# Norms by blocks of two and four tiles, squares of the residual added up by TensorE, S5 tables without zero blocks

## The chip, the cores and the metric

The kernel runs on one core of one Trainium2 chip. The metric is the time of one execution in microseconds (us) on the device. The kernel is written in Bass with the Tile framework, whose scheduler gives every engine its list of instructions from the program's order and from priorities.

## The reference

The program is one inference step of a decoder of two layers, on a prompt of 512 tokens and on 8 sequences of 4 new tokens that share the weights; the width D is 1024. Each layer is:

```
h = rms_norm(x, g_mix_pre)
p = h @ w_in                      # split into four head groups
m = concat(rwkv7(p1), s5(p2), gated_delta(p3), sliding_window_attention(p4))
x = x + rms_norm(m @ w_out, g_mix_post)
h = rms_norm(x, g_mlp_pre)
x = x + rms_norm(square(relu(h @ w_up)) @ w_down, g_mlp_post)

def rms_norm(x, g):
    return x * lax.rsqrt(jnp.mean(x * x, axis=-1, keepdims=True) + 1e-6) * g
```

The S5 group is a complex diagonal state space model: 16 groups of 16 channels, 64 states each, with input and output matrices B and C for each group. The outputs are the two results and all states of the four mixers.

## The kernel before

**Halves.** The 544 columns (tokens) are worked off in two halves: half 0 has 256 columns of the prompt, half 1 the other 256 and the 32 columns of the samples, 288. A vector x is kept transposed, as 8 tiles of 128 rows (features) by n columns; a norm's sum over features is therefore a sum over tiles on one engine, and then over partitions by a product with `mean`, a column of 1/D that is broadcast to 128x128.

**Dense products.** `dense` goes over units of 128 output rows. A unit's weights come in two half-units [128, 4, 128] (`load_part`, issued by SP, line 1658, five buffers `wraw`). ScalarE rounds each to `whi`, VectorE subtracts to get `wlo` (three buffers each), the input is split likewise (`h[0]`, `h[1]`), and three products (hi*hi, hi*lo, lo*hi) over eight tiles make 24 matmuls a unit. All matmuls have the one line 219 (`mm`). The other helpers are `tt` (two tensors, line 235), `stt` (tensor, scalar, tensor, line 244), `act` (line 227) and `acopy` (line 231, copies and casts on ScalarE).

**Norms.** `square_sum` squares one tile on ScalarE and has GpSimd add it to `sums`; `rms` multiplies by `mean` and takes the root on ScalarE (Ln, then Exp). `prenorm` makes h for the next dense product: for each of 8 tiles one `stt` (x times weight times root), one cast, one subtraction. `residual` does for each tile one `stt` (output times weight times root), one `tt` (add the old x, which comes by DMA from DRAM, one tile at a time into the class `xk`), and `square_sum` of the new x; in the last layer it takes whole buffers. Its temporaries and the squares share the class `d1`, two buffers.

**S5.** `s5_tables` makes for each layer the tables kin, m1 and m2 and stores them in DRAM; `s5_main`, once for each half and layer, loads them (`halves`, `table`, line 1439, classes r4 and r2, five buffers each) and forms products of 128x128 blocks with the inputs U and the states H. Two groups of 64 rows share a block, and the blocks off the diagonal hold zeros. A float32 matmul shows as two instructions of TensorE.

**Order.** `body` writes out the order: project and mixers of a half, `out_proj`, `mlp`. A residual is put into `pending` (`later`) and popped inside the next dense product, ahead of its second and third unit, with the priority 'norm'; `flush` pops at once. Thus mix (0,0) is the residual after the output projection of layer 0, half 0, and mlp (0,1) that after the MLP of layer 0, half 1. There are eight: mix and mlp for two layers and two halves; mlp (1,0) and (1,1) are final and write the result.

**Buffers.** `CLS` gives each class its bytes per partition and its buffers: h9, f9 and acc are whole inputs of 8 tiles, two buffers each; xs has one. h9 holds the inputs of projections and of the MLP, f9 the MLP's inner activations or the input of the next layer's projection.

Of the kernel before, what the change touches and what calls it, by code (L numbers as in the profile page):

```python
# [9 lines left out]
F32 = mybir.dt.float32  # L10
# [9 lines left out]
HA = 288  # L20
# [4 lines left out]
NORM_EPS, RW_LN_EPS = 1e-6, 64e-5  # L25

# [112 lines left out]
class K:  # L139
# [21 lines left out]
    CLS = {"c0": (640, 7), "c1": (1152, 4), "e1": (1280, 2), "d1": (1152, 2), "xk": (1152, 3), "sums": (1152, 3),  # L161
# [1094 lines left out]
    def s5_tables(self, l):  # L1256
# [51 lines left out]
        misc = self.w([128, 2, 512], "r4")  # L1308
        bx, cx = (self.view(misc[:, j], [128, 2, 8, 2, 16]) for j in range(2))
# [14 lines left out]
        for out, pq, a, b, c, d in ((kx, rv, bb[:, 0], bb[:, 1], bb[:, 1], bb[:, 0]),  # L1324
                                    (m1, pw[:, :, 1:5], bc[:, 1, 0], bc[:, 1, 1], nbc[:, 1], nbc[:, 0])):
            for x, (u, v) in enumerate(((a, b), (c, d))):
                for y, w in enumerate((u, v)):
                    self.tt(tmp[:, y], over(w), pq[:, y].rearrange("q j a -> q a j").unsqueeze(2).to_broadcast([128, 8, 16, 4]), eng=e)
                for g2 in range(2):
                    rs = slice(64 * g2, 64 * g2 + 64)  # L1330
                    self.tt(out[x][rs, :, g2], tmp[rs, 0], tmp[rs, 1], ALU.add if x else ALU.subtract, eng=e)
        for g2 in range(2):
            rs = slice(64 * g2, 64 * g2 + 64)
            for x in range(2):
                nc.gpsimd.tensor_copy(bx[rs, x, :, g2], bb[rs, x])
            nc.gpsimd.tensor_copy(cx[rs, 0, :, g2], bc[rs, 1, 0])
            nc.gpsimd.tensor_copy(cx[rs, 1, :, g2], nbc[rs, 1])
        tab = [self.t([128, n], f"s5{nm}{l}", pool="dram", bufs=1) for nm, n in (("kin", 2048), ("m1", 2048), ("m2", 1024))]
        for x in range(2):
            self.nc.sync.dma_start(out=tab[1][:, x * 1024:x * 1024 + 1024], in_=m1[x].rearrange("p a b c d -> p (a b c d)"))  # L1340

        gps = []
        for q in range(2):
            gp = self.ps([128, 4, 2, 4, 16])
            for e in range(4):
                w = 4 * q + e
                for x in range(2):
                    lt = bx[:, x, w].rearrange("p a c -> p (a c)")
                    self.mm(gp[:32, e, :, 0], lt, cx[:, x, w], x == 0, False)
                    self.mm(gp[:32, e, :, 1:4], lt, m1[x][:, w, :, :, 0:3].rearrange("p g h j -> p g j h"), False, x == 1)  # L1350
            gps.append(gp)
        ga = self.w([32, 8, 2, 4, 16], "s0")
        for q in range(2):
# [680 lines left out]
```

## Time and profile before

| | |
|---|---|
| median of 3 runs | 1672.88 us (1667.75 to 1679.4) |
| profiled execution | 1675.07 us, span 1673.3 us, mean granted clock of TensorE 0.966 |
| TensorE | 1576.6 us busy, 94% of the span |
| VectorE | 1245.0 us, 74% |
| ScalarE | 952.2 us, 57% |
| GpSimd | 373.9 us, 22% |
| read from and written to HBM | 243.20 MB, 31.21 MB |

PE is TensorE's matmul part, PEld its weight load, DVE VectorE, ACT ScalarE, POOL GpSimd, SP the engine that issues most DMAs. A busy time is the union of an engine's instructions; the mean of one instruction overlaps its neighbours on TensorE, so there the busy time divided by the count, or the distance of two starts, is what one costs.

### The profile page before, as it was taken

Reading aid. Unit: us, or ns where it says so; the run is one execution under the profiler, and the core shown is the slowest. Engines: PE = TensorE matmul, PEld = TensorE weight load, DVE = VectorE, ACT = ScalarE, POOL = GpSimd, SP = SyncE. Lnnn points to the kernel's source line nnn. Section 1 sums busy time; section 2 is a strip of 40 time slices with the busy share of each in tenths; the row PEclk is TensorE's granted clock in tenths of the full one; section 3 lists DMA queues with packets and bytes.
Section 4 is the critical chain, followed back from the end, with each engine's and each line's share of the span. In section 5 each row is a group of like instructions: output and inputs, shape, how many; then the busy total and the mean of one; then the engine's idle time right before and its main releaser. Section 6 shows DMA issues by size and latency. Waiting matters only on the chain. (4 is left out here: it accounts for less than half of the span.)

```text
span 1673.3 us, 38301 instructions
## 1 busy us (share of the span) xinstructions
PE 1576.6 (94%) x14098; PEld 1472.2 (88%) x14098; DVE 1245.0 (74%) x3067; ACT 952.2 (57%) x2096; POOL 373.9 (22%) x689
## 2 busy tenths in 40 slices
PE   6988998789999999989999998999999999899996
PEld 6877987679898999879989998989899899899996
DVE  7888675876696868898576667989778865966665
ACT  5676556744346467765453556886444456655543
POOL 6561142200122614530001004530002101400002
PEclk9998998879999999999999999999999899999998
DMA  6634453343467557736346455535544765555452
GB/s 219 221 120 118 140 165 123 108 119 117 135 189 252 179 170 231 234 105 167 106 152 196 165 179 191 172 126 144 145 140 146 234 209 187 194 189 166 160 169 98
DMA packets 210184, 275.21 MB, mean 164 GB/s; under 512 B 78266, under 2 KB 101116, under 8 KB 209580
## 3 DMA queue, kind: packets, MB, share of 16 engines
q1 hardware_dynamic: 208076, 266.59, 50.8%
q0 software_dynamic: 1920, 6.17, 1.0%
q8 instruction: 110, 1.80, 0.4%
q14 instruction: 78, 0.64, 0.1%
HBM read 243.20 MB, written 31.21 MB: 164 GB/s over the span
## 5 line engine op out<-in xcount | busy, mean ns | idle before, releaser
L231 ACT CAST whi<-wraw 128x512 fp32r<-128x512 f32 x752 | 463.5, 619 | 439.3 <-PE ps L219 268.4
L235 DVE TENSOR_TENSOR wlo<-wraw,whi 128x512 fp32r<-128x512 f32 x752 | 545.7, 730 | 198.5 <-ACT whi L231 171.3
L219 PE MATMUL ps<-h,whi 128*128 128x288 f32 (+1 forms) x3264 | 518.6, 299 | 20.1 <-ACT h L231 17.8
L219 PEld LDWEIGHTS ps<-h,whi 128*128 128x128 f32 x3264 | 455.4, 194 | 35.2 <-ACT h L231 22.1
L219 PE MATMUL ps<-f,whi 128*128 128x288 f32 (+1 forms) x2752 | 425.6, 294 | 9.6 <-ACT whi L231 4.7
L219 PEld LDWEIGHTS ps<-f,whi 128*128 128x128 f32 x2752 | 374.4, 190 | 22.4 <-ACT whi L231 6.8
L219 PE MATMUL ps<-h,wlo 128*128 128x288 f32 (+1 forms) x1632 | 291.0, 298 | 7.4 <-DVE wlo L235 6.8
L219 PEld LDWEIGHTS ps<-h,wlo 128*128 128x128 f32 x1632 | 238.7, 193 | 16.1 <-DVE wlo L235 11.2
L219 PE MATMUL ps<-f,wlo 128*128 128x288 f32 (+1 forms) x1376 | 238.7, 293 | 3.3 <-DVE wlo L235 3.1
L235 POOL TENSOR_TENSOR sums<-sums,d 128x288 f32<-128x288 f32 (+1 forms) x105 | 101.8, 970 | 548.9 <-ACT d L227 541.0
L219 PEld LDWEIGHTS ps<-f,wlo 128*128 128x128 f32 x1376 | 197.4, 190 | 8.5 <-DVE wlo L235 4.6
L219 PE MATMUL ps<-r,r 128*128 128x72 f32 (+7 forms) x800 | 90.0, 281 | 4.5 <-DVE r L235 2.6
L219 PEld LDWEIGHTS ps<-r,r 128*128 128x128 f32 (+4 forms) x800 | 72.3, 175 | 11.0 <-DVE r L235 3.3
L235 DVE TENSOR_TENSOR acc<-acc,ps 128x256 f32<-128x256 f32 (+1 forms) x96 | 41.7, 434 | 49.5 <-PE ps L219 49.1
L231 ACT CAST f<-d 128x256 fp32r<-128x256 f32 (+1 forms) x136 | 56.6, 416 | 29.1 <-DVE d L235 28.5
L227 ACT ACTIVATE d<-acc 128x288 f32<-128x288 f32 (+1 forms) x109 | 46.2, 431 | 34.5 <-DVE acc L235 20.9
L235 DVE TENSOR_TENSOR f<-d,f 128x256 fp32r<-128x256 f32 (+1 forms) x136 | 59.1, 436 | 6.8 <-ACT f L231 6.7
L235 DVE TENSOR_TENSOR d<-d 128x288 f32<-128x288 f32 (+1 forms) x128 | 58.1, 454 | 0.7 <-ACT d L227 0.7
L227 ACT ACT_TABLE_LOAD x43 | 55.2, 1283 | 0.8
L227 ACT ACTIVATE d<-ps 128x288 f32<-128x288 f32 (+1 forms) x128 | 50.4, 394 | 8.8 <-PE ps L219 8.0
L244 DVE SCALAR_TENSOR_TENSOR d<-acc,pf,sums 128x256 f32<-128x256 f32 (+1 forms) x80 | 39.7, 507 | 6.2 <-ACT sums L227 4.9
L231 ACT COPY r<-ps 64x128 f32<-64x128 f32 (+2 forms) x60 | 22.7, 383 | 27.3 <-PE ps L624 11.4
(381 smaller groups left out, 1861.9 us busy)
## 6 DMA issues: line engine op xcount, KB each, us to landing
wraw<-in_w_up SPq DMA_DIRECT2D x256, 256.0 KB, 2.8
wraw<-in_w_down SPq DMA_DIRECT2D x256, 256.0 KB, 2.9
wraw<-in_w_in SPq DMA_DIRECT2D x176, 256.0 KB, 3.0
wraw<-in_w_out SPq DMA_DIRECT2D x64, 256.0 KB, 2.9
r<-s5m SPq DMA_DIRECT2D x12, 512.0 KB, 5.2
t<-diag SPq DMA_DIRECT2D x32, 128.0 KB, 3.2
r<-s5kin SPq DMA_DIRECT2D x8, 512.0 KB, 5.2
x<-acc SPq DMA_DIRECT2D x3, 1152.0 KB, 5.5
```

What stands on the lines that cost most here:

```text
L219: return self.nc.tensor.matmul(out=out, lhsT=lhsT, rhs=rhs, start=start, stop=stop)
L227: return self.nc.scalar.activation(out=out, in_=in_, func=func, scale=scale, bias=bias, **kw)
L231: return self.nc.scalar.copy(out, in_)
L235: return (eng or self.nc.vector).tensor_tensor(out=out, in0=a, in1=b, op=op)
L244: return self.nc.vector.scalar_tensor_tensor(out=out, in0=a, scalar=s, in1=b, op0=op0, op1=op1)
```

## The change

Five things change. (1) `prenorm` multiplies blocks of two tiles by the root on VectorE; ScalarE then applies the weight while it rounds, and VectorE's `stt` gives the low part. (2) `residual` works on blocks of four tiles (two where it is final), takes x in two DMAs of four tiles into a larger class, and the weights g_mix_post and g_mlp_post are applied before it, by ScalarE, in `out_proj.out` and in `mlp.down`. (3) For five of the six residuals that are not final, ScalarE squares blocks of four tiles and eight products with `mean` add them up, and no GpSimd add is left there. In all other sums the add of the last tile goes to VectorE. (4) S5's tables have no zero blocks any more, and their products are made in two 64x64 quadrants. (5) The table building works on the smaller tables.

```diff
@@ CLS
-"xk": (1152, 3)
+"d2": (2304, 2)
@@ s5_tables
-        kx, m1 = ([self.w([128, 8, 2, 16, 4], "r4") for _ in range(2)] for _ in range(2))
-        for tl in (*kx, *m1, bx, cx):
-            nc.gpsimd.memset(tl, 0.0)
+        kx, m1 = (self.w([128, 2, 8, 16, 4], "r4") for _ in range(2))
+        nc.gpsimd.memset(bx, 0.0)
...
-                for g2 in range(2):
-                    rs = slice(64 * g2, 64 * g2 + 64)
-                    self.tt(out[x][rs, :, g2], tmp[rs, 0], tmp[rs, 1], ALU.add if x else ALU.subtract, eng=e)
+                self.tt(out[:, x], tmp[:, 0], tmp[:, 1], ALU.add if x else ALU.subtract, eng=e)
...
-                    self.mm(gp[:32, e, :, 0], lt, cx[:, x, w], x == 0, False)
-                    self.mm(gp[:32, e, :, 1:4], lt, m1[x][:, w, :, :, 0:3].rearrange("p g h j -> p g j h"), False, x == 1)
+                self.mm(gp[:32, w, 0], lt, (bc[:, 1, 0] if not x else nbc[:, 1])[:, w], x == 0, False)
+                self.mm(gp[:32, w, 1:4], lt, m1[:, x, w, :, 0:3].rearrange("p h j -> p j h"), False, x == 1)
...
-                for e in range(4):
-                    self.tr(tp[:, e], kx[x][:, 4 * q + e].rearrange("p a b c -> p (a b c)"))
-                self.acopy(kin[:, 4 * q:4 * q + 4], tp)
-            self.nc.sync.dma_start(out=tab[0][:, x * 1024:x * 1024 + 1024], in_=kin.rearrange("p a c -> p (a c)"))
+            for q in range(4):
+                self.tr(tp[:, q], kx[:, x, 2 * q:2 * q + 2].rearrange("p a b c -> p (a b c)"))
+            kin = self.w([128, 4, 128], "r2")
+            self.acopy(kin, tp)
+            for e in range(2):
+                for g2 in range(2):
+                    self.nc.sync.dma_start(out=kt[64 * g2:64 * g2 + 64, x, :, e], in_=kin[64 * e:64 * e + 64, :, 64 * g2:64 * g2 + 64])
...
@@ s5_main
-        kin = halves(tkin)
+        kin = table(self.w([128, 2, 8, 64], "r4"), tkin)
-                    self.mm(p[:, e], kin[g0 // 4][:, x, e], U[:, g0 + e])
+                    for rs in GROUPS:
+                        self.mm(p[rs, e], kin[rs, x, g0 + e], U[rs, g0 + e])
-        m1, m2 = halves(tm1), table(self.w([128, 8, 128], "r4"), tm2)
+        m1, m2 = table(self.w([128, 2, 8, 64], "r4"), tm1), table(self.w([128, 8, 64], "r2"), tm2)
-                self.mm(yp[:, e], m2[:, w], U[:, w], True, False)
+                for rs in GROUPS:
+                    self.mm(yp[rs, e], m2[rs, w], U[rs, w], True, False)
                 for x in range(2):
-                    self.mm(yp[:, e], m1[g0 // 4][:, x, e], H[x][:, w], False, x == 1)
+                    for rs in GROUPS:
+                        self.mm(yp[rs, e], m1[rs, x, w], H[x][rs, w], False, x == 1)
@@ square_sum
-        self.tt(sums, sums, sq, ALU.add, eng=self.nc.gpsimd)
+        self.tt(sums, sums, sq, ALU.add, eng=self.nc.gpsimd if m < 7 else None)
@@ prenorm
-        for k in range(8):
-            t = self.row(half, "c1" if half and self.last_layer else "d1")
-            self.stt(t, x[:, k], self.p(g)[:, k:k + 1], rs)
-            self.parts(h[0][:, k], h[1][:, k], t)
+        for q in range(0, 8, 2):
+            u = self.w([128, 2, HA], "r2" if half and self.last_layer else "d2")[:, :, :n]
+            self.tt(u, x[:, q:q + 2], rs.unsqueeze(1).to_broadcast([128, 2, n]))
+            for k in (q, q + 1):
+                gk = self.p(g)[:, k:k + 1]
+                self.act(h[0][:, k], u[:, k - q], AF.Copy, scale=gk)
+                self.stt(h[1][:, k], u[:, k - q], gk, h[0][:, k].bitcast(F32), ALU.mult, ALU.subtract)
@@ residual
+    def fetch(self, half, cls):
+        if cls == "r4":
+            xt = [self.w([128, 4, HALVES[half][1]], "r4") for _ in range(2)]
+        else:
+            t = self.big(half, cls)
+            xt = [t[:, 0:4], t[:, 4:8]]
+        for q in range(2):
+            self.nc.sync.dma_start(out=xt[q], in_=self.x[half][:, 4 * q:4 * q + 4])
+        return xt
...
-            t = self.row(half, "c1" if whole else "d1")
-            self.stt(t, src[:, k], self.p(g)[:, k:k + 1], rs)
-            self.tt(src[:, k], t, xk, ALU.add, eng=self.nc.gpsimd if final and k % 2 else None)
-            if not final:
-                self.square_sum(new, k, src[:, k])
+        step = 2 if final else 4
+        for q in range(0, 8, step):
+            a, xq = src[:, q:q + step], xt[q // 4][:, q % 4:q % 4 + step]
+            self.tt(a, a, rs.unsqueeze(1).to_broadcast([128, step, n]))
+            self.tt(a, a, xq, ALU.add, eng=self.nc.gpsimd if final and q == 2 else None)
+            if final:
+                self.nc.sync.dma_start(out=self.o["yT"][:, q:q + step, c0:c0 + n], in_=a)
+            elif wide:
+                self.act(xq, a, AF.Square)
+                mp = self.ps([128, n], "mn") if mp is None else mp
+                for k in range(4):
+                    m = self.mm(mp, self.mean.to_broadcast([128, 128]), xq[:, k], q + k == 0, q + k == 7)
             else:
+                for k in range(4):
+                    self.square_sum(new, q + k, a[:, k])
...
-        return new
+        return self.rsqrt(new, mp, m) if wide else self.rms(new)
@@ out_proj.out
-            self.acopy(o[:, m], ps)
-            self.square_sum(sums, m, o[:, m])
+            self.square_sum(sums, m, ps)
+            self.act(o[:, m], ps, AF.Copy, scale=self.p("g_mix_post")[:, m:m + 1])
@@ out_proj
+        cls = {(0, 0): "f9", (0, 1): "h9", (1, 0): "r4", (1, 1): "xs"}[l, half]
+        self.later(lambda: x.update(rs=self.residual(half, o, sums, cls, wide=(l, half) != (0, 1))))
@@ mlp.down, after the last sum of squares
+                self.act(acc[:, m], acc[:, m], AF.Copy, scale=self.p("g_mlp_post")[:, m:m + 1])
@@ mlp
+        self.later(lambda: r.update(s=self.residual(half, acc, sums, ("xs" if half else "r4") if final else "f9", final)))
```

## Rows read from the trace of the kernel before

**Rows 1.** The page, part 1: engine, busy us, share of the span, instructions.

```profile
PE 1576.6 (94%) x14098; PEld 1472.2 (88%) x14098; DVE 1245.0 (74%) x3067; ACT 952.2 (57%) x2096; POOL 373.9 (22%) x689
```

**Rows 2.** Waits of PE: what for, us in total, times, longest.

```profile
PE ps L219 <- ACT h L231: 17.8, 10, 3.6
...
PE ps L219 <- POOL sums L235: 7.9, 3, 4.4
...
PE ps L219 <- DMA r<-s5m: 1.2, 1, 1.2
```

**Rows 3.** Windows: length, busy us of PE, PEld, DVE, ACT, POOL; clock, DMA, GB/s.

```profile
340.00:360.00 20.00, 17.57 (x111) 14.55 (x112) 17.17 (x68) 6.82 (x17) 0.56 (x1) 0.51 0.38 97
1040.00:1060.00 20.00, 15.98 (x95) 14.53 (x94) 17.92 (x36) 15.99 (x42) 9.29 (x14) 0.83 0.45 138
1300.00:1320.00 20.00, 17.13 (x107) 16.41 (x108) 14.26 (x49) 5.05 (x12) 4.85 (x5) 0.80 0.88 297
1440.00:1460.00 20.00, 15.94 (x98) 15.11 (x99) 18.04 (x33) 14.13 (x30) 10.17 (x11) 0.83 0.66 217
```

**Rows 4.** Lines by form, PE: tile, array part, size, count, busy us, mean ns.

```profile
L219 PE MATMUL ps<-t,t 64*64 64x64 f32 x1024 | 37.2, 224 | 1.0 <-DMA t<-diag 1.0
L219 PE MATMUL ps<-r,r 128*128 128x72 f32 x160 | 21.6, 297 | 1.2 <-DMA r<-s5m 1.2
...
L219 PE MATMUL ps<-r,r 128*32 128x96 f32 x64 | 13.5, 342 | 0.3 <-DVE r L235 0.2
```

**Rows 5.** Timeline of PE, S5's products: start, us, operation, [idle before it].

```profile
225.15 2.00 PE L219 MATMUL ps<-r,r 128*128 128x64 f32 x16
227.07 0.74 PE L219 MATMUL ps<-g,g 64*64 64x64 f32 x20
...
483.49 5.47 PE L219 MATMUL ps<-r,r 128*128 128x72 f32 x48
488.76 0.95 PE L219 MATMUL ps<-f,whi 128*128 128x256 f32 x6
```

**Rows 6.** Timeline of PE around the norm after mlp (0,1).

```profile
1039.00 0.65 PE L219 MATMUL ps<-sums,mean 128*128 128x288 f32 x2
1039.27 0.86 PE L219 MATMUL ps<-h,wlo 128*128 128x256 f32 x4
1039.96 1.10 PE L219 MATMUL ps<-h,whi 128*128 128x256 f32 x8
1040.90 0.63 PE L219 MATMUL ps<-h,wlo 128*128 128x256 f32 x4
1045.13 1.01 PE L219 MATMUL ps<-f,whi 128*128 128x288 f32 x4 [3.60 <-ACT f L231]
```

**Rows 7.** Timeline there, DVE's last residual adds and POOL's sums.

```profile
1033.34 0.81 DVE L235 TENSOR_TENSOR acc<-c,xs 128x288 f32<-128x288 f32 x2
...
1032.52 6.14 POOL L235 TENSOR_TENSOR sums<-sums,d 128x288 f32<-128x288 f32 x4 [2.46 <-ACT d L227]
```

**Rows 8.** Timeline after mix (0,0): last residual add, first normed product.

```profile
336.87 0.41 DVE L235 TENSOR_TENSOR acc<-d,xk 128x256 f32<-128x256 f32 x1
...
342.36 1.23 PE L219 MATMUL ps<-h,whi 128*128 128x256 f32 x4 [1.97 <-ACT h L231]
```

**Rows 9.** Lines by form: operations of wide blocks, and a scaled copy.

```profile
L235 DVE TENSOR_TENSOR cv<-cv,g 128x1152 f32<-128x1152 f32 x2 | 2.7, 1348 | 0.0
...
L235 DVE TENSOR_TENSOR r<-r,r 128x576 f32<-128x576 f32 x4 | 3.0, 756 | 1.9 <-ACT r L227 1.9
...
L227 ACT ACTIVATE xs<-ps,rwd 128x256 f32<-128x256 f32 x18 | 9.1, 506 | 0.0
```

**Rows 10.** Timeline of the tail, PE and DVE.

```profile
1659.88 1.16 PE L219 MATMUL ps<-sums,mean 128*128 128x288 f32 x2 [2.02 <-POOL sums L235]
...
1662.15 2.35 DVE L244 SCALAR_TENSOR_TENSOR c<-acc,pf,sums 128x288 f32<-128x288 f32 x4 [3.80 <-ACT sums L227]
...
1668.01 1.41 DVE L235 TENSOR_TENSOR acc<-c,xs 128x288 f32<-128x288 f32 x2
```

More of the change, by code (lines that the diff above doesn't have):

```diff
@@ L1307, in s5_tables @@
         self.tt(k(9), k(9), k(6))
-        misc = self.w([128, 2, 512], "r4")
-        bx, cx = (self.view(misc[:, j], [128, 2, 8, 2, 16]) for j in range(2))
+        bx = self.w([128, 2, 8, 2, 16], "r4")
         bb2 = self.w([128, 2, 2, 8, 16], "r2")
@@ L1621, in residual @@
-    def residual(self, half, src, sums, g, final=False):
+        for q in range(0, 8, 2):
[5 more added lines that the diff above has]
+                self.stt(h[1][:, k], u[:, k - q], gk, h[0][:, k].bitcast(F32), ALU.mult, ALU.subtract)
@@ L1623, in residual @@
+        return h
+    def fetch(self, half, cls):
[7 more added lines that the diff above has]
+        return xt
+    def residual(self, half, src, sums, cls, final=False, wide=True):
         c0, n = HALVES[half]
+        xt = self.fetch(half, cls)
@@ L1624, in residual @@
         rs = self.rms(sums)
-        new = self.row(half, "sums")
-        whole = self.last_layer and (half or final)
-        if whole:
-            xw = self.big(half, "xs") if half else [self.w([128, 4, n], "r4") for _ in range(2)]
-            xw = [xw[:, k] for k in range(8)] if half else [xw[k // 4][:, k % 4] for k in range(8)]
-            for k in range(8):
-                self.nc.sync.dma_start(out=xw[k], in_=self.x[half][:, k])
-        for k in range(8):
-            if whole:
-                xk = xw[k]
-            else:
-                xk = self.row(half, "xk")
-                self.nc.sync.dma_start(out=xk, in_=self.x[half][:, k])
-            t = self.row(half, "c1" if whole else "d1")
-            self.stt(t, src[:, k], self.p(g)[:, k:k + 1], rs)
-            self.tt(src[:, k], t, xk, ALU.add, eng=self.nc.gpsimd if final and k % 2 else None)
-            if not final:
-                self.square_sum(new, k, src[:, k])
-            elif k % 2:
-                self.nc.sync.dma_start(out=self.o["yT"][:, k - 1:k + 1, c0:c0 + n], in_=src[:, k - 1:k + 1])
+        step = 2 if final else 4
@@ new lines, in residual @@
+        new = None if final else self.row(half, "sums")
+        mp = None
+        for q in range(0, 8, step):
[9 more added lines that the diff above has]
+                    m = self.mm(mp, self.mean.to_broadcast([128, 128]), xq[:, k], q + k == 0, q + k == 7)
+            else:
+                for k in range(4):
+                    self.square_sum(new, q + k, a[:, k])
@@ L1779, in mlp @@
         r = {}
-        self.later(lambda: r.update(s=self.residual(half, acc, sums, "g_mlp_post", final)))
+        self.later(lambda: r.update(s=self.residual(half, acc, sums, ("xs" if half else "r4") if final else "f9", final)))
         if not final:
             self.pf = self.pfs[l + 1]
-            self.later(lambda: r.update(h=self.prenorm(half, acc, "g_mix_pre", self.rms(r["s"]), "f9")))
+            self.later(lambda: r.update(h=self.prenorm(half, acc, "g_mix_pre", r["s"], "f9")))
             self.pf = self.pfs[l]
```

56 lines of the change are left out of this document (21 added, 35 removed).

## The prediction

> **What bounds the kernel now.** I read the profile's page first, then the waits of TensorE, the 20-us windows, the lines kept apart by form, and timelines around the places found so. The page [rows 1]: TensorE is busy 94% of the span, VectorE 74%, ScalarE 57%, GpSimd 22%. A microsecond is gained where TensorE gets less to do, or where it stands still; work taken from the others counts only there. The waits of TensorE [rows 2] say where it stands still for what the diff touches: 17.8 us for the norm's output `h`, 7.9 us for the sums of squares that GpSimd adds, 1.2 us for the S5 table `r<-s5m`. The windows [rows 3] show that a stall costs twice. At 1040, 1300 and 1440 us TensorE's granted clock is 0.83, 0.80 and 0.83 of full over 20 us, so 3.4, 4.0 and 3.4 us of clock are lost after stalls of 3.6 us or less; at 340 us it is 0.51 of 2.4 GHz, so near the lower of its two levels, 1.2 GHz, the whole time. The sum is made against the profiled execution: 1675.07 us, of which 1673.3 are its span; it lies 0.13% above the median 1672.88.
>
> **S5's products.** A call of s5_main makes 40 full 128x128 products, each two instructions, so 80. Forty-eight of them with 72 columns take 488.76 - 483.49 = 5.27 us at the full clock, 0.110 each [rows 5], 8.8 us a call. The new ones are 80 products in 64x64 quadrants, 160 instructions. The row nearest is `t,t 64*64 64x64`: 37.2 us of busy time for 1024, 0.036 each [rows 4]. With 64 columns a call is 160 x 0.036 = 5.8, with 72 columns 160 x 0.041 = 6.5. Two calls of each: 2 x 3.0 + 2 x 2.3 = 10.6; the slow stretches make the old ones dearer (21.6 us over 160, 0.135 each [rows 4]), so I take **-11**. Bounds: going from 64x64 to 128x128 and back costs 225.15 to 227.07, 1.92 us, less 16 x 0.110, so 0.16 [rows 5]. Were each of the 24 groups of products cut out of dense work, that is +3.8; the low end is -15, if all were at the slow price.
>
> Here a rule speaks against it. In that row two quadrants write one bank and an instruction still costs 0.036 [rows 4]. The Trainium skill's TensorEngine Tiling (Array Packing), Restrictions and Gotchas, says that different row tiles cannot use one PSUM bank at the same time, and the new lines write both halves of `p[rs, e]` in one bank. By that rule the pair would run one after the other; the row does not agree, if its two quadrants count as such. By the row the term is -11, by the rule near nothing. It is a rival below.
>
> **S5's tables.** The products into `gp` go from 96 to 48 and from 32 to 16 columns; the 64 with 96 columns are busy 13.5 us [rows 4], so half of that is at most -6.7. Half of the 32 transposes go, 16 x 0.110 = -1.8, with 0.110 borrowed from the S5 products [rows 5]. Memsets of six 4-KB tiles become one, the adding operations run over 128 partitions instead of twice 64, half the bytes are stored, but kin's store becomes eight transfers a layer instead of two on SP. This lies beside dense work. I take **-5**, between -8.5 and 0.
>
> **Squares of the residual on TensorE.** Of the eight residuals two are final; five of the other six are `wide`: eight products with `mean` in place of one, 35 more. The price is read at 1039 us [rows 6]: eight dense instructions take 1039.96 to 1040.90, 0.94; the product with `mean` and four dense take 1039.00 to 1039.96, 0.96; less 0.47 leaves 0.49 at 288 columns, 0.435 at 256. Fourteen of the 35, for mix (1,0) and mlp (0,0), fall where TensorE has dense work waiting: 14 x 0.435 = **+6**. The other 21 lie at the three stalls below and are in their terms. Were all to count, +16.
>
> **Stall after mlp (0,1), 1045 us.** The last adds of the residual end at 1033.34 + 0.81 = 1034.15 on VectorE; GpSimd's sums end at 1032.52 + 6.14 = 1038.66 [rows 7]. So sums lag 4.5 us; the product with `mean` comes at 1039.00, and TensorE later stands still 3.60 us for `f`, the norm's output [rows 6]. With the squares of four tiles on ScalarE (near 1.2 us, taken like the 1.35 of VectorE for 1152 columns [rows 9]) and the sum on TensorE, about 3 us of the lag goes, and blocks of two shorten the norm a little: 3.6 of stall and 3.4 of lower clock, less 7 x 0.49 = 3.4 for the products. **-3.5**; bounds -7 (products in the idle time) and +3.4 (ScalarE busy with weights, nothing gained).
>
> **Stall after mix (1,1), 1449 us.** The same pattern: longest wait for `h` 3.6 [rows 2], clock 0.83 [rows 3]: **-3.5**, same bounds.
>
> **Stall after mix (0,0), 340 us.** Last add on VectorE 336.87, first product with the normed `h` 342.36 [rows 8]; between stand GpSimd's add, `mean` (TensorE waits up to 4.4 for it [rows 2]), ScalarE's root and the first norm tiles. The residual's 16 instructions of at least 0.41 (6.6 us) become four of 1024 columns at 1.35 x 1024/1152 = 1.2 (4.8) [rows 8, 9]; about 1 us goes with GpSimd's add; but the clock is halved, so the last four products with `mean` cost some 4 x 0.87 = 3.5 where one was. Together near nothing on the chain; but the residual is spread over other VectorE work, and with whole blocks it can come earlier, into time in which TensorE is idle. **-3**, between -9 and +3.
>
> **S5's table load at 1300 us.** TensorE waits 1.2 for `r<-s5m` [rows 2] and the window runs at 0.80 [rows 3], 4.0 lost. m1 and m2 come from three transfers of 512 KB into three r4 buffers; now one of them and one of half the size, in one r4 and one r2. The stall goes with half of the bytes and one buffer less to wait for. **-4**, of 0 to -5.2.
>
> **Tail.** Before: last matmul, square, GpSimd's add, `mean` at 1659.88 (2.02 of wait for that add), VectorE from 1662.15 to 1669.42 [rows 10]. GpSimd's add of m = 7 goes to VectorE, a few tenths sooner; then seven VectorE operations of 576 columns at 0.756 [rows 9] are 5.3 instead of 7.3, with one of GpSimd's between. **-1.5**; 0 to -2.4.
>
> **What costs nothing.** In mlp.down 32 scaled copies are new; the nearest row with a scale pointer is 0.506 [rows 9], 16 us of a ScalarE that is 57% busy [rows 1]. Four-tile operations of 1.35 us hold up VectorE's splits of the weights; the cover is three buffers of split weights, some 3 x 12 x 0.117 = 4 us of dense work. Without the cover each such hold would be a wait of a few tenths. The fetches of x are the same bytes on SP in two transfers instead of eight.
>
> The sum: -11 - 5 + 6 - 3.5 - 3.5 - 3 - 4 - 1.5 = -25.5, that is 1675.07 - 25.5 = 1649.6, rounded **1650**. Its own range goes half of the way to the low bounds (22.6 in all) and a third of the way to the high ones (about 44): 1638 to 1664.
>
> **Rivals.**
> (a) *The waits are refilled.* VectorE is busy 17.9 and 18.0 of 20 us in the windows at 1040 and 1440 [rows 3], so ends that GpSimd no longer delays may be delayed by splits of weights and by ScalarE's new copies. Then only TensorE's work counts, with all 35 products: -11 - 5 + 16 = 0, so 1675. Against it: VectorE loses work there too, and GpSimd's lag is plain in rows 7.
> (b) *The two quadrants wait for each other.* Were a pair of instructions as long as one full one, 160 x 0.055 = 8.8 us, the old price, the first term would be gone: 1650 + 11 = 1661. For it: only the bank both write. Against it: the row at 0.036 [rows 4].
> (c) *Slower: the fetch of x holds SP.* x now goes into a whole f9 buffer (mix (0,0), mlp (0,0), mlp (0,1)) or h9 (mix (0,1)), which comes free only after the last product of the matmuls that read it. SP issues in order; behind the fetch stand the next loads of weights, and five raw buffers are 5 x 12 x 0.117 = 7 us of dense work. A fetch that waits W costs W - 7. A block of eight units is 8 x 24 x 0.117 = 22.5 us, so four fetches cost at most 4 x 15.5 = 62, and 1650 + 62 = 1712. It decides, past 1% slower, once the four cost 42 together, each waiting over 17 us. Against it: the products that free these buffers stand ahead in program order, so most are done when the residual is popped from `pending`, one or two units later; and each of the rows of TensorE's waits that I took [rows 2] names a norm, a sum or a table, none a fetch of x.
>
> **How the numbers follow.** Chances: forecast 0.62, (a) 0.22, (b) 0.05, (c) 0.11. About 1% is what a measurement of this kernel tells from no change: 1656 to 1690 around the median. The forecast is faster: 0.62 (the part of its own range above 1656 is set against runs of (a) that end below it). (a) and (b) are within 1%: 0.27. (c) is slower: 0.11. The range: downwards, all low bounds together (-15 - 8.5 + 6 - 7 - 7 - 9 - 5.2 - 2.4 = -48.1) give 1627; upwards it takes in (b) and (a) and the lighter part of (c), to 1682.
>
> **What would show it.** Right: 64x64 products of S5, 640 in all, at a pitch near 0.04; GpSimd's `sums` at 60 instead of 105; 35 more products with `mean` or their squares; waits for `h` and `f` at the three stalls under 2 us each and the clock there above 0.9; no wait for `r<-s5m`; the tail after `mean` near 9 us instead of 11. Wrong: the same waits under another name (VectorE `u`, ScalarE's copies), SP waiting over 7 us at the fetch of x with TensorE waiting for splits behind it, or S5's pitch near 0.055 or more.

## The result and the profile after

The changed kernel takes 1648.79 us, the median of 4 runs (1643.43 to 1656.59); the kernel before 1672.12 (4 runs). The ratio is 0.9851, with an interval of 0.9816 to 0.9885. The profiled execution of after took 1651.66 us, its span is 1649.9, 23.4 us shorter than the span of before. The prediction was 1650. The total came out as forecast; the table of stretches below shows that it did not come about as the sum had it.

The page of after (engines; the granted clock in 40 slices), and the waits of PE that answer to [rows 1, 2]:

```profile
PE 1562.9 (95%) x14472; PEld 1458.9 (88%) x14472; DVE 1216.6 (74%) x2959; ACT 964.7 (58%) x2094; POOL 312.8 (19%) x614
...
PEclk9999998999999999999999999999999999999998
```

```profile
PE ps L220 <- DVE wlo L236: 11.5, 14, 3.0
PE ps L220 <- DVE d L236: 9.2, 2, 8.1
PE ps L220 <- ACT whi L232: 8.8, 9, 3.4
PE ps L220 <- ACT h L228: 4.6, 3, 2.3
PE ps L220 <- ACT f L228: 4.4, 1, 4.4
...
PE ps L220 <- DMA r<-s5m: 3.1, 2, 1.9
...
PE ps L220 <- DVE sums L236: 2.1, 2, 1.6
```

The waits for the norm's output `h` fell from 17.8 to 4.6 us (a further 1.7 stand under a cast) and those under the name of GpSimd's sums are gone. But at the norm after mix (0,0), where TensorE waited 4.4 us for the sums [rows 2], it now waits 4.4 for `f`, ScalarE's squares: the same stall under another name. 2.1 us for the last add, now VectorE's, remain. The 9.2 us for `d` belong to the first norm of all, whose products with `mean` waited in the kernel before too: 7.2 us, 4.7 of them under the name of a GpSimd operation. `wlo` and `whi` cost about 2 us more each. The wait for the S5 table did not go: 3.1 us instead of 1.2.

The windows around the places of [rows 3], at their new times, and one at 680 us that had no row before:

```profile
320.00:340.00 20.00, 15.63 (x93) 12.14 (x95) 18.15 (x58) 11.86 (x26) 0.56 (x1) 0.78 0.35 90
680.00:700.00 20.00, 14.56 (x90) 13.45 (x91) 15.97 (x31) 7.83 (x20) 7.43 (x16) 0.83 0.41 134
1020.00:1040.00 20.00, 19.34 (x145) 18.59 (x144) 16.45 (x29) 16.93 (x43) 5.94 (x13) 1.00 0.53 180
1300.00:1320.00 20.00, 16.59 (x130) 15.85 (x130) 16.36 (x60) 13.17 (x33) 0.00 (x0) 1.00 0.59 191
1420.00:1440.00 20.00, 18.50 (x138) 17.52 (x138) 15.99 (x29) 15.76 (x34) 2.72 (x3) 1.00 0.67 231
```

At the stalls after mlp (0,1) and mix (1,1), windows 1020 and 1420, the clock is full (0.83 before); after mix (0,0) it is 0.78 and then full, where it was 0.64 and then 0.51. At 680 us there is a new place with a clock of 0.83.

The forms of [rows 4] in after:

```profile
L220 PE MATMUL ps<-r,r 64*64 64x64 f32 x448 | 17.0, 221 | 1.9 <-DVE t L248 1.5 <-POOL r L236 0.4
...
L220 PE MATMUL ps<-r,r 64*64 64x72 f32 x320 | 12.7, 228 | 3.1 <-DMA r<-s5m 3.1
...
L220 PE MATMUL ps<-f,mean 128*128 128x256 f32 x32 | 9.2, 438 | 4.4 <-ACT f L228 4.4
...
L220 PE MATMUL ps<-r,r 128*32 128x48 f32 x64 | 7.8, 257 | 0.2 <-DVE r L236 0.2
```

S5's products are the 320 with 72 columns and 320 of the 448 with 64 (128 of that form were there before). An instruction costs 0.040 and 0.038 us of busy time.

**Where the time went.** TensorE's 9024 dense matmuls (those with split weights) are the same in every kernel here and start in the same order, so the trace can be cut at the start of the same one. I worked this table out from these starts, one profiled execution a kernel; spans in us. Each kernel in it is described under Experiments. Stretch A runs from the start of the span to matmul 1152 (projections and mixers of layer 0, half 0), B to 1344 (the stall after mix (0,0)), C to 4224 (the rest of layer 0's half 1, mlp (0,0), the table building and projection of layer 1), D to 5184, E to 5472 (the stall after mlp (0,1)), F to 7680 (S5's last table load and the stall after mix (1,1)). The 1344 matmuls after that take 178.2 to 178.7 in all kernels.

| kernel | A | B | C | D | E | F | time, median |
|---|---|---|---|---|---|---|---|
| before | 294 | 84 | 526 | 129 | 49 | 397 | 1672 to 1675 |
| after | 288 | 70 | 534 | 131 | 43 | 394 | 1648.8 |
| S5 parts alone | 284 | 80 | 525 | 129 | 49 | 401 | 1667.4 |
| norms alone | 312 | 69 | 550 | 131 | 43 | 391 | 1681.6 |
| before, load 310 | 300 | 87 | 526 | 129 | 49 | 407 | 1687.0 |
| S5 parts alone, load 310 | 289 | 72 | 528 | 129 | 49 | 394 | 1655.0 |
| after, load 310 | 282 | 72 | 544 | 131 | 43 | 395 | 1659.2 |
| after, load 280 | 286 | 68 | 542 | 131 | 43 | 385 | 1649.5 |
| norms alone, load 280 | 305 | 66 | 550 | 131 | 43 | 391 | 1682.2 |
| sums on GpSimd | 289 | 69 | 541 | 138 | 40 | 397 | 1666.5 |
| single tiles | 290 | 70 | 547 | 131 | 43 | 394 | 1666.8 |
| all six wide | 286 | 70 | 532 | 131 | 43 | 389 | 1641.5 |
| quadrants in series | 286 | 68 | 538 | 131 | 43 | 395 | 1655.3 |
| en on GpSimd's queue | 292 | 70 | 532 | 131 | 43 | 390 | 1645.4 |

How much of a stretch is the execution's own scatter shows in the last row against after: one DMA stands in another queue, the order is the same but for a few instructions, and A and F still differ by 5 and 4 us. The profiled execution isn't always near the median either: that of norms alone took 1689.3 us and that of before at 310 1693.6, each the slowest of its kernel, and their rows add up accordingly.

Small products of the mixers can also cross a cut. In B of the kernel before there are 104 instructions of them (64x64 products and a few transposes, 3.8 us of TensorE) that lie in C of after. So part of what B loses C gains, and the two are best read together: 610.1 us before, 603.6 after.

### The profile page after: what moved, and what is told of

It reads as the page before. It is cut to its first block, busy times and chain, and to the rows that moved or that the text cites. A ratio compares the mean times of both kernels' runs of the same rounds, so it can differ in the third digit from the quotient of the medians.

```text
span 1649.9 us, 38760 instructions
## 1 busy us (share of the span) xinstructions
PE 1562.9 (95%) x14472; PEld 1458.9 (88%) x14472; DVE 1216.6 (74%) x2959; ACT 964.7 (58%) x2094; POOL 312.8 (19%) x614
## 3 DMA queue, kind: packets, MB, share of 16 engines
q0 software_dynamic: 1920, 6.17, 1.0%
## 5 line engine op out<-in xcount | busy, mean ns | idle before, releaser
L236 DVE TENSOR_TENSOR wlo<-wraw,whi 128x512 fp32r<-128x512 f32 x752 | 537.6, 721 | 215.1 <-ACT whi L232 187.2
L220 PE MATMUL ps<-h,whi 128*128 128x288 f32 (+1 forms) x3264 | 517.4, 298 | 12.7 <-ACT whi L232 6.0
L236 POOL TENSOR_TENSOR sums<-sums,d 128x288 f32<-128x288 f32 (+1 forms) x60 | 61.1, 1019 | 537.1 <-ACT d L228 532.9
L232 ACT CAST f<-d 128x288 fp32r<-128x288 f32 (+1 forms) x128 | 53.4, 417 | 35.7 <-DVE d L236 35.5
L220 PE MATMUL ps<-r,r 64*64 64x64 f32 (+7 forms) x1184 | 68.3, 237 | 6.3 <-DMA r<-s5m 3.1
L220 PEld LDWEIGHTS ps<-r,r 64*64 64x64 f32 (+4 forms) x1184 | 56.6, 140 | 15.5 <-issue 8.0
L228 ACT ACTIVATE d<-ps 128x256 f32<-128x256 f32 (+1 forms) x156 | 61.4, 394 | 13.3 <-PE ps L220 11.4
L236 DVE TENSOR_TENSOR f<-d,f 128x288 fp32r<-128x288 f32 (+1 forms) x128 | 55.4, 434 | 1.9 <-ACT f L232 1.7
L232 ACT COPY e<-ps 128x256 f32<-128x256 f32 (+2 forms) x96 | 28.0, 325 | 18.1 <-PE ps L220 8.5
L220 PE MATMUL ps<-t,t 64*64 64x64 f32 x1024 | 36.5, 221 | 2.0 <-DMA t<-diag 2.0
L220 PEld LDWEIGHTS ps<-t,t 64*64 64x64 f32 x1024 | 32.6, 135 | 6.2 <-DMA t<-diag 2.4
```

Of the source, the lines that this page charges most:

```text
L220: return self.nc.tensor.matmul(out=out, lhsT=lhsT, rhs=rhs, start=start, stop=stop)
L228: return self.nc.scalar.activation(out=out, in_=in_, func=func, scale=scale, bias=bias, **kw)
L232: return self.nc.scalar.copy(out, in_)
L236: return (eng or self.nc.vector).tensor_tensor(out=out, in0=a, in1=b, op=op)
```

## Experiments

The first four split the change and undo one part of it.

**S5 parts alone (s5_only).** In the kernel before, s5_tables and s5_main are those of the changed kernel; the core of it:

```diff
+GROUPS = (slice(0, 64), slice(64, 128))
...
-        kin = halves(tkin)
+        kin = table(self.w([128, 2, 8, 64], "r4"), tkin)
...
-                    self.mm(p[:, e], kin[g0 // 4][:, x, e], U[:, g0 + e])
+                    for rs in GROUPS:
+                        self.mm(p[rs, e], kin[rs, x, g0 + e], U[rs, g0 + e])
...
```

> The kernel before with the S5 tables and products of the changed one alone (parts 4 and 5); norms, residuals and sums as before. Theory (the terms add up as in the prediction, S5's products costing what the changed kernel's rows show): products 40 to 22 us, tables -5 at most, the table load's stall partly: -18 to -24 us, so 1648 to 1654. Rival (the S5 work lies beside waits for VectorE, and the time is set by the norms): -5 us or less, over 1667. The stalls after mix (0,0) stay: waits of PE for the sums of GpSimd over 6 us in all.

1667.36 us, ratio 0.9948 (0.9931 to 0.9966): 5 to 9 us faster (before's median lay between 1672 and 1675 from one set of runs to the next). Between theory and rival, and too little for the theory.

**Norms alone (norms_only).** The changed kernel with the old s5_tables and s5_main; the core of it:

```diff
-        kin = table(self.w([128, 2, 8, 64], "r4"), tkin)
+        kin = halves(tkin)
...
-                    for rs in GROUPS:
-                        self.mm(p[rs, e], kin[rs, x, g0 + e], U[rs, g0 + e])
+                    self.mm(p[:, e], kin[g0 // 4][:, x, e], U[:, g0 + e])
...
```

> The changed kernel with the S5 tables and products of the kernel before (zero blocks and whole 128x128 products); parts 1 to 3 stay. Theory: the stalls after mix (0,0), mlp (0,1), mix (1,1) and the tail give back 14 + 6 + 3 + 2 us and the products with the mean take some 6: -12 to -18 us, 1654 to 1660. Rival (refilled: the freed waits return as waits for split weights, and 35 products more take 13 us): within 5 us of before, over 1667.

1681.56 us, ratio 1.0053 (1.0032 to 1.0074): slower. That is no gain, so the theory failed; it is over 1667, as the rival said, but 7 to 9 us above before instead of within 5. The two parts give some -8 and +8 and together -23 or more, so their prices don't add up. The timeline of PE, ACT and VectorE at 247 to 259 us shows the largest loss:

```profile
258.45 1.33 PE L220 MATMUL ps<-e,cst 128*128 128x288 f32 x2 [9.39 <-ACT e L232]
...
257.49 0.31 ACT L228 ACTIVATE gde<-gdx 128x16 f32<-128x16 f32 x2 [8.98 <-DVE gdx L236]
...
247.06 2.87 DVE L1493 TENSOR_TENSOR_SCAN r<-r,r 128x512 f32<-128x512 f32 x2
249.85 1.26 DVE L236 TENSOR_TENSOR r<-r,r 128x512 f32<-128x512 f32 x2
...
251.64 2.48 DVE L236 TENSOR_TENSOR r<-r,r 128x512 f32<-128x512 f32 x2
254.04 1.74 DVE L236 TENSOR_TENSOR wlo<-wraw,whi 128x512 fp32r<-128x512 f32 x1
255.70 0.23 DVE L236 TENSOR_TENSOR gdx<-ps,cst 128x16 f32<-128x16 f32 x2
```

TensorE stands still 9.39 us for a copy `e` on ScalarE; ScalarE waited 8.98 us at the head of its list for `gdx`, and VectorE comes to `gdx` at 255.70 only after S5's scans and products. Two of these (`r<-r,r` at 251.64) take 1.24 us each while GpSimd works, where the two before them, with GpSimd idle, take 0.63 each; that GpSimd is the cause was not tried. In the kernel before the scans stand ahead of `gdx` too, and TensorE's longest wait for an `e` is 1.8 us. Why it has nothing else to do at this moment here was not settled; the 64x64 products `t,t` of this half, for one, begin at 166.0 us instead of 148.2. No operation of a norm is among these rows.

**Sums on GpSimd (sums_gpsimd).**

```diff
     def residual(self, half, src, sums, cls, final=False, wide=True):
+        wide = False
```

> The changed kernel, but no residual adds its squares on TensorE: single tiles squared on ScalarE and added on GpSimd, the last on VectorE, one product with the mean. Theory (GpSimd's lag of 4.5 us at the stalls is what TensorE waited for): the 35 products and their 13 us of TensorE go, but the stalls at the norms after mix (0,0), mlp (0,1) and mix (1,1) come back with their lower clock, 4 to 8 us each: about +5 us against the changed kernel, 1651 to 1660. Rival (the blocks were the gain, the products are a cost): -6 to -12 us against it, 1637 to 1643.

1666.45 us, ratio 0.9939 (0.9918 to 0.996), some 17 us above the changed kernel: the sign of the theory, three times its size. The waits of PE and two places of its timeline:

```profile
PE ps L220 <- DVE sums L236: 17.9, 5, 8.3
...
632.51 1.22 PE L220 MATMUL ps<-sums,mean 128*128 128x256 f32 x2 [6.17 <-DVE sums L236]
...
1027.98 1.33 PE L220 MATMUL ps<-sums,mean 128*128 128x288 f32 x2 [8.34 <-DVE sums L236]
```

The sums are waited for 17.9 us in all, 8.34 at the norm after mlp (0,1) and 6.17 at the one after mlp (0,0). VectorE's add is the last of a chain of which six stand on GpSimd:

```profile
1020.59 6.85 POOL L236 TENSOR_TENSOR sums<-sums,d 128x288 f32<-128x288 f32 x6 [13.84 <-ACT d L228]
```

The kernel before, with its sums on GpSimd as well, had no wait for them at these two places (after mlp (0,1) it waited 3.60 us for `f` instead [rows 6]). There the tiles came one by one and GpSimd's adds ran beside them; here a block gives four squares at once and the adds follow in one chain. So in the changed kernel the products with `mean` are worth more than they cost, but a part of what they save seems to be a wait that the blocks would bring; no run has the new norms with single tiles and GpSimd's sums. In the table D and E together are 177.4 to 177.9 in the four kernels with the old norms, 177.8 here, and 173.0 in after: at mlp (0,1) the gain comes and goes with the products.

**The table en on another queue (en_store).**

```diff
-        self.nc.sync.dma_start(out=ten, in_=en.rearrange("p x a c -> p (x a c)"))
+        self.nc.gpsimd.dma_start(out=ten, in_=en.rearrange("p x a c -> p (x a c)"))
```

> The changed kernel with one transfer on another queue: the store of S5's table en goes from SP's to GpSimd's queue. In the changed kernel's profile SP stands 8.8 us ahead of that store, waiting for GpSimd's arithmetic at 685 us, and TensorE waits 3.0 and 2.4 us for weights at 683 and 689 us at a clock of 0.83. Theory (the store holds the loads behind it): those waits go, -5 to -10 us against the changed kernel, 1639 to 1644. Rival (TensorE waits there for VectorE, busy with the norm and the convolution): no change, 1646 to 1652.

1645.4 us, ratio 0.9823 (0.9793 to 0.9853), against 0.9851 (0.9816 to 0.9885): not told apart. The rows at the place, first of after (PE, then SP's waits), then of the experiment:

```profile
683.68 1.02 PE L220 MATMUL ps<-f,wlo 128*128 128x256 f32 x4 [3.01 <-DVE wlo L236]
...
689.70 1.21 PE L220 MATMUL ps<-f,whi 128*128 128x256 f32 x8 [2.43 <-ACT cv L228]
...
SPq L1393 <- POOL r L236: 12.2, 2, 8.8
```

```profile
688.89 1.22 PE L220 MATMUL ps<-f,wlo 128*128 128x256 f32 x4 [3.02 <-DVE wlo L236]
```

The wait of 2.43 is not there when the store is on the other queue, the one of 3.0 for VectorE's `wlo` stands. At most a few us come from the queue here; the larger wait is VectorE's, as the rival had it.

**Quadrants in series (quad_serial).**

```diff
-                for e in range(4):
-                    for rs in GROUPS:
+                for rs in GROUPS:
+                    for e in range(4):
                         self.mm(p[rs, e], kin[rs, x, g0 + e], U[rs, g0 + e])
...
-            for e in range(4):
-                w = g0 + e
-                for rs in GROUPS:
-                    self.mm(yp[rs, e], m2[rs, w], U[rs, w], True, False)
-                for x in range(2):
-                    for rs in GROUPS:
-                        self.mm(yp[rs, e], m1[rs, x, w], H[x][rs, w], False, x == 1)
+            for rs in GROUPS:
+                for e in range(4):
+                    w = g0 + e
+                    self.mm(yp[rs, e], m2[rs, w], U[rs, w], True, False)
+                    for x in range(2):
+                        self.mm(yp[rs, e], m1[rs, x, w], H[x][rs, w], False, x == 1)
```

> The changed kernel; in S5's two sets of products all of the first quadrant's products come first and then all of the second's, instead of both in turn for each block. Theory (two quadrants overlap although they write one bank): the last 80 instructions of a call, 2.48 to 2.65 us in the changed kernel (0.031 to 0.033 each), take 0.055 or more each, over 4.4 us; four calls with 640 instructions +15 us at most on TensorE, perhaps +5 to +12 on the time. Rival (one bank, so they never ran together): 0.031 to 0.036 each as before, no change of the time beyond what another order of instructions makes.

1655.25 us, ratio 0.9887 (0.9847 to 0.9927): 6 us above after, where the theory had it, but the intervals overlap. The pitch decides. The timelines of PE, consecutive products of a call's second set, of after and of the experiment, both at the full clock:

```profile
241.42 2.55 PE L220 MATMUL ps<-r,r 64*64 64x64 f32 x80
243.90 0.40 PE L220 MATMUL ps<-h,whi 128*128 128x288 f32 x1
...
471.04 2.72 PE L220 MATMUL ps<-r,r 64*64 64x72 f32 x80
473.69 0.51 PE L220 MATMUL ps<-f,whi 128*128 128x256 f32 x2
```

```profile
239.61 4.80 PE L220 MATMUL ps<-r,r 64*64 64x64 f32 x88
244.35 0.54 PE L220 MATMUL ps<-cst,c 16*128 16x8 f32 x4
```

In turn, 80 instructions take 243.90 - 241.42 = 2.48 us, 0.031 each, and 2.65 with 72 columns, 0.033. In series 88 take 244.35 - 239.61 = 4.74, 0.054 each. The first set of a call, in which no product adds to another's result, agrees: 16 instructions with 72 columns take 0.65 us in turn (after, 1267.51) and 0.95 in series (experiment, 1270.55). So two quadrants run side by side though both write one PSUM bank, and the order in which they are written out is what makes them do so.

**Single tiles (one_tile).**

```diff
-            self.tt(a, a, rs.unsqueeze(1).to_broadcast([128, step, n]))
-            self.tt(a, a, xq, ALU.add, eng=self.nc.gpsimd if final and q == 2 else None)
+            if final:
+                self.tt(a, a, rs.unsqueeze(1).to_broadcast([128, step, n]))
+                self.tt(a, a, xq, ALU.add, eng=self.nc.gpsimd if q == 2 else None)
+            else:
+                for k in range(step):
+                    self.tt(a[:, k], a[:, k], rs)
+                    self.tt(a[:, k], a[:, k], xq[:, k], ALU.add)
```

> The changed kernel; in the residuals that are not final VectorE works on single tiles again (8 products with the root and 8 adds instead of 2 and 2), squares and products with the mean stay as they are. Theory (what was gained after mix (0,0) and mlp (0,1) came from GpSimd's add leaving the chain): +2 to +5 us against the changed kernel, since 12 more starts of VectorE cost about 2 us in each of six places, most of them hidden. Rival (the blocks made the gain): the 14 us after mix (0,0) and 6 after mlp (0,1) are lost in good part, +10 to +20 us.

1666.81 us, ratio 0.994 (0.9916 to 0.9964): the size of the rival, but not at its places. B and E of the table stay at 70 and 43, so neither of these stalls returns; the loss of 13 us is in C. What the blocks gain they gain there, or the order does; this run does not tell which. The place after mix (0,0):

```profile
318.76 2.75 DVE L236 TENSOR_TENSOR acc<-acc,sums 128x256 f32<-128x256 f32 x8
321.52 0.41 DVE L236 TENSOR_TENSOR acc<-acc,f 128x256 f32<-128x256 f32 x1
...
322.20 2.42 DVE L236 TENSOR_TENSOR acc<-acc,f 128x256 f32<-128x256 f32 x7
...
335.04 2.41 PE L220 MATMUL ps<-h,whi 128*128 128x256 f32 x14 [0.93 <-ACT h L228]
```

The sixteen single operations are done in 322.20 + 2.42 - 318.76 = 5.9 us, with little of other work between them.

**The same instructions in another order.** After this the question was whether parts have prices at all here. One number in the priorities reorders the work and changes no instruction:

```diff
-PRIO = {'rw1': 500, 'gd1': 200, 'rw2': 392, 'gd2': 3000, 'rwt': 300, 's5': 5486, 'gd3': 140, 'sws': 200, 'norm': 800, 'evac': 1050, 'load': 294, 'mix': 1500, 'gdt': 200}
+PRIO = {'rw1': 500, 'gd1': 200, 'rw2': 392, 'gd2': 3000, 'rwt': 300, 's5': 5486, 'gd3': 140, 'sws': 200, 'norm': 800, 'evac': 1050, 'load': 310, 'mix': 1500, 'gdt': 200}
```

In two of the runs the number is 280.

after_load310: 

> The changed kernel with the same instructions and another number in the scheduler's priorities (loads of weights 310 instead of 294), so that only the order changes. If the order alone moves the time by 8 us or more either way, the -8.7 of the S5 parts alone and the +8.9 of the norms alone are not prices of the parts but of the orders that came with them. If it stays within 4 us of the changed kernel (1645 to 1653), the two parts need each other for another reason.

norms_load280: 

> The kernel with the new norms alone, again with another number in the priorities only (280 instead of 294). It took 1681.6 us, 26 of them more than the kernel before between 190 and 312 us and around 700 us, while the stalls after mix (0,0), mlp (0,1), mix (1,1) and the tail were gone. If that loss is of the order, the time falls to 1655 to 1672; if the new norms cost it in any order, it stays over 1676.

before_load310: 

> The kernel before with the load priority 310 instead of 294: same instructions, another order. If an order is worth about 10 us either way, as in the changed kernel (+10.4), this comes out at 1662 to 1684 and moves by 5 us or more; if the kernel before is as it was in any order, 1670 to 1678.

s5_load310: 

> The kernel before with the S5 parts alone, load priority 310. Against the kernel before with the same priority the S5 parts should give 15 to 23 us if their work is the price (18 us less of S5's products, 5 of tables); -9 again, as at 294, if a part of the freed time always goes to other waits.

after_load280: 

> The changed kernel, load priority 280: a third order of the same instructions. If 294 is a chosen good order, this is slower, 1653 to 1662, as 310 was; if orders scatter evenly, 1640 to 1660 with either sign.

| kernel | 280 | 294 | 310 |
|---|---|---|---|
| before | | 1672 to 1675 | 1687.0 (1.0091: 1.0061 to 1.012) |
| S5 parts alone | | 1667.4 | 1655.0 (0.9894: 0.9868 to 0.992) |
| norms alone | 1682.2 (1.0059: 1.0035 to 1.0083) | 1681.6 | |
| after | 1649.5 (0.9864: 0.9836 to 0.9893) | 1648.8 | 1659.2 (0.9898: 0.9856 to 0.9939) |

In brackets is the ratio to the kernel before at 294. The order alone moved before by +15 and the S5 parts alone by -12, both clear of noise; it moved after by +10 with 310, where the intervals just overlap, and not at all with 280. So the orders scatter, and 294 is not the one good order of after. The S5 parts are worth 5 to 9 us in one order and 32 in the other, more than the 15 to 23 expected; the norms on top of them 19 in one and -4 in the other. Norms alone stayed over 1676, the sign that its expectation gave for a cost of the norms in any order: both orders are slow in A and C. But 280 changed the order less than 310 did in the other kernels, so one more order is thin evidence for it.

**All six residuals wide (all_wide).**

```diff
-        self.later(lambda: x.update(rs=self.residual(half, o, sums, cls, wide=(l, half) != (0, 1))))
+        self.later(lambda: x.update(rs=self.residual(half, o, sums, cls)))
```

> The changed kernel, with the sixth residual, mix (0,1), also adding its squares on TensorE. In the changed kernel GpSimd takes 3.24 us for one add at 650 us there, beside its S5 arithmetic, and TensorE loses 7.4 us in the 83 us that follow (1.9 in the kernel before). Theory (the add on GpSimd is late wherever GpSimd has other work): 7 more products, 3.4 us, and 5 to 9 us of stalls less: -2 to -6 against the changed kernel, 1643 to 1647. Rival (the stalls there are VectorE's, the products come on top): +2 to +5, 1651 to 1654.

1641.53 us (1635.35 to 1649.33), ratio 0.9813 (0.9768 to 0.9859): the fastest of all, 31 us below before. It lies below the theory's 1643, but its interval overlaps with that of after, so the two are not told apart by time. The window at the place that the expectation named differs plainly:

```profile
680.00:700.00 20.00, 19.39 (x155) 18.08 (x154) 13.88 (x35) 15.43 (x37) 1.88 (x8) 1.00 0.48 146
```

TensorE is busy 19.39 of 20 us at the full clock, where after had 14.56 at 0.83. But C is 532 us in this run and 532 also with en on GpSimd's queue, where no norm was changed; so a gain in time is not shown.

## Why the prediction was right in the total, and where it was not

**S5's products: the mechanism right, the size too small.** Forecast -11 from a price of 0.036 and 0.041; the rows give 0.038 and 0.040. But the old ones cost 40.3 us of busy time [rows 4; 21.6 for 72 columns and, by the same view, 18.7 for 64] and the new 12.7 and 17.0 less the 5.2 of the 128 others, 24.5: -15.8 of TensorE's busy time, just past the low bound of -15. The new price was met; the old one was taken too low, at the pitch of the full clock for every call (35.2 for the four). Forty-eight of the old ones ran largely at the lower clock after the stall for the table (8.29 us for what takes 5.27 at the full clock [rows 5]):

```profile
1309.51 8.29 PE L219 MATMUL ps<-r,r 128*128 128x72 f32 x48 [1.16 <-DMA r<-s5m]
```

The rival that two quadrants wait for each other is refuted by 0.031 against 0.054. It came from the Trainium skill, TensorEngine Tiling (Array Packing), Restrictions and Gotchas, that row tiles can't use a PSUM bank at the same time; here they do, or with no cost that the pitch shows, and the measurement decides.

**S5's tables.** The products into `gp` with 96 columns went from 13.5 to 7.8 us, -5.7, close to the bound of -6.7. Those that went from 32 to 16 columns hardly changed, 7.6 to 7.4, and the transposes of this kind fell from 12.8 to 10.5. Together that is -8.2 of busy time, near the low bound, where the sum had -5.

**Products with the mean.** Two calls with 256 columns take 9.2 us of busy time, 4.6 each, one of them in the slow stretch after mix (0,0); the forecast was 8 x 0.435 = 3.5 at the full clock. So the price held. But I counted 14 of them as +6 of pure cost. Taking them out (sums on GpSimd) made the kernel slower by 17 us and brought a wait of 6.17 us at mlp (0,0), one of the two places where I had counted them as cost alone. What I did not see is that blocks of four tiles, summed on GpSimd, come with a wait that the kernel before, with its single tiles, does not have.

**The stall after mlp (0,1).** E is 48.7 to 49.1 in all four kernels with the old norms and 42.5 to 43.0 in the nine that have the new norms with sums on TensorE: -6, while D, with its products, is 1 to 3 longer; together -5, and sums on GpSimd gives it all back. The sum had -3.5 for the stall and +3 for the products of mix (1,0), which lie in E too. This is the one term of the norms that every order confirms. How it was to be seen, too: waits and clock of [rows 6, 3] against window 1020 at 1.00.

**The stall after mix (1,1).** TensorE's wait of 3.59 us for `h` is gone and the clock is full in the window at 1420, as the term of -3.5 had it. F, where it lies together with S5's last products and their table load, is only 3 us shorter.

**The stall after mix (0,0): the step that failed.** The sum had -3, with -9 as its end; B gave -14. VectorE's first step in before, then of after its blocks and TensorE's products, then a window of before and one of after:

```profile
323.09 0.88 DVE L244 SCALAR_TENSOR_TENSOR d<-acc,pf,sums 128x256 f32<-128x256 f32 x2
```

```profile
316.86 2.34 DVE L236 TENSOR_TENSOR acc<-acc,sums 128x1024 f32<-128x1024 f32 x2
...
319.55 2.34 DVE L236 TENSOR_TENSOR acc<-acc,f 128x1024 f32<-128x1024 f32 x2
...
322.49 3.50 PE L220 MATMUL ps<-f,mean 128*128 128x256 f32 x8 [4.39 <-ACT f L228]
...
331.13 3.24 PE L220 MATMUL ps<-h,whi 128*128 128x256 f32 x14 [1.21 <-ACT h L228]
```

```profile
320.00:340.00 20.00, 7.67 (x64) 5.13 (x62) 17.57 (x59) 11.46 (x32) 7.55 (x9) 0.64 0.43 110
```

```profile
340.00:360.00 20.00, 20.00 (x286) 17.93 (x282) 18.00 (x59) 11.03 (x30) 0.00 (x0) 1.00 0.33 109
```

B has three pieces. Up to VectorE's first step it is 29 us in both kernels. From there to TensorE's first product with the normed h it is 342.36 - 323.09 = 19.3 us in before [rows 8] and 331.13 - 316.86 = 14.3 in after: -5.0. From that product to the end of B it is 35.9 and 26.1: -9.8. In this last piece the kernel before runs at a clock of 0.51 until 360 us [rows 3], and after at 1.00 from 340. The prediction read the 0.51 and used it to price the four last products with `mean`, but it counted nothing for the clock that comes back, where it counted 3.4 us at each of the other two stalls. Nor is all of the 9.8 clock: the 104 small instructions that went to C are 3.8 us of it.

For the 5.0 the operations were costed rightly: the four blocks take 2.34 + 2.34 = 4.7 us (forecast 4.8). What was not costed is what stands between: in before VectorE's work for attention and delta rule lies between the residual's steps. That blocks can't be cut into is not the reason that it no longer does, for the single tiles of one_tile stand as close, and B is 70 there; nor is it the sums, for with sums on GpSimd B is 69. What these kernels share, and before has not, is that the steps write in place, without the two buffers of `d1` that the squares hold too, and that x comes in two transfers and the weight is applied earlier. None of these was undone alone, so the cause stays open. The S5 parts alone, with the old norms, reach 72 in B in one order, and 80 in the other.

Two signs of being right failed here: the wait for `f` is 4.39 us, not under 2, and the clock is 0.78 at 320 us, not above 0.9.

**What the sum had no term for.** C is 525 to 528 us in the four kernels with the old norms and 532 to 550 with the new ones, +4 to +25, in every order. With B added, which gives work to C in some of them, the two groups overlap: 600 to 614 and 601 to 619. So it is not shown that the norms cost time here. In C lie mlp (0,0), mix (0,1), GpSimd's table building and layer 1's projection, and 8 of the 32 new copies of `mlp.down`, 4 us of ScalarE by [rows 9]. GpSimd's single adds of mix (0,1) go beside its S5 arithmetic there, and one took 3.24 us:

```profile
650.40 3.24 POOL L236 TENSOR_TENSOR sums<-sums,d 128x288 f32<-128x288 f32 x1 [2.54 <-ACT d L228]
...
653.93 1.25 POOL L236 TENSOR_TENSOR sums<-sums,d 128x288 f32<-128x288 f32 x1
```

With all_wide C is 2 us shorter than in after, no more than scatter; what C costs stays open, and no run tells whether ScalarE's copies, which I had costed at nothing because that engine is 57% busy, are part of it.

**The table load at 1300 us.** The sum had -4. The stall for `r<-s5m` did not go (1.16 at one place and 1.89 at another), the clock there is now full, and a wait of 3.41 us for `whi` came behind the fetch of x, which SP issued at 1287.50. In en_store, with the same order of these transfers, that wait is not there, so it is no fixed price of the fetch. Rival (c), a fetch that holds SP for over 17 us at four places, was not seen: SP's longest wait at a fetch of x is 3.5 us.

**Tail.** Forecast -1.5. From the start of the last product with the mean VectorE needs 1669.42 - 1659.88 = 9.5 us [rows 10] in before, and in after 1644.16 + 2.08 - 1638.00 = 8.2. Counted from the last dense matmul to the end, so with the sums ahead of that product, the tail is 1.9 us shorter.

```profile
1638.00 0.75 PE L220 MATMUL ps<-sums,mean 128*128 128x288 f32 x2 [1.64 <-DVE sums L236]
...
1640.27 3.96 DVE L236 TENSOR_TENSOR acc<-acc,sums 128x576 f32<-128x576 f32 x4 [2.33 <-ACT sums L228]
1644.16 2.08 DVE L236 TENSOR_TENSOR acc<-acc,xs 128x576 f32<-128x576 f32 x3
```

**So** the total was met by errors that cancel, and in part by luck. If the terms are laid where their rows lie (an estimate from the prediction's own figures), the sum had some -5.5 in A, -8 in B and C together, -0.5 in D and E, -10 in F and -1.5 in the tail. The two profiled executions gave -6.6, -6.5, -4.9, -3.4 and -1.9. B and C together look right only because B gave 11 us more than its term and C 13 less. D and E gave over 4 us more and F over 6 less, where A and F scatter by 4 to 5 us from one execution to the next. Rival (a), refilled waits, is what happens in one order (after at 310 gains nothing over the S5 parts at 310) and not in the other; it should have had its chance from the order, not from VectorE's load. What stays open is why the orders with norms alone begin the delta rule 18 us later, and whether C costs more work or only holds more of it.

## What to carry to other kernels

Where a scheduler places every instruction anew, a part's measured effect is a price plus the worth of one order; vary a priority that changes no instruction, in both kernels, before a difference of 1% is put down to a part. A cost that all orders show at the same place (the stall after mlp (0,1), the pitch of the quadrants) can be trusted. When a chain of small operations of a high priority is cut into by other work, cost what stands between its steps and not only the steps, and count the time at the lower clock behind a stall as well as the stall. Where a trace is cut at the same matmul in two kernels, other work can cross the cut; read neighbouring stretches together. Products that share a PSUM bank in two quadrants are worth writing in turn.

## What the runs showed of the hardware

Two 64x64 quadrants on the diagonal, written in turn into one PSUM bank, overlap: 0.031 to 0.033 us an instruction against 0.054 in series and 0.110 for a full 128x128 one of 64 or 72 columns. A GpSimd add of 128x288 numbers that takes about 1.0 us by itself took 3.24 at 650 us in after, where VectorE ran blocks of 1152 columns and weight splits beside it; that this is the cause was not tried.
